# A two-layer decoder trunk: inputs stored in DRAM in the chip's own order

## The chip, the cores and the metric

The kernel runs on one core of a Trainium2 chip. The metric is the time of one execution on the device in microseconds (us), the median of several runs. TensorE is called PE here, its weight loads PEld, VectorE DVE, ScalarE ACT, GpSimd POOL, SyncE SP.

## What is computed

The input is 512 tokens of 1024 features; 16 learned meta tokens are put in front, so T = 528. Two layers follow, each a token mixer and a gated FFN with a causal convolution of width 3, all with residual adds and RMS norms, in float32:

```python
h = concat([meta_tokens, x])                        # (528, 1024)
h = h + diff_attention(rms_norm(h, da_norm), ...)   # 8 heads, two softmaxes each, rope, w_qkv 1024x3072, w_o
h = h + conv_ffn(rms_norm(h, ffn_norm[0]), ...)     # w_up 1024x5632, conv, silu gate, w_down 2816x1024
h = h + dsa_attention(rms_norm(h, dsa_norm), ...)   # indexer picks top keys per query; 16 heads; w_in 1024x3656, w_o
h = h + conv_ffn(rms_norm(h, ffn_norm[1]), ...)
return rms_norm(h, final_norm)[16:]                 # (512, 1024)
```

## The kernel before

**Layout.** The residual stream lies on the chip with features on partitions: eight tiles `h[0]` to `h[7]` of 128 x 528. A projection multiplies weight slabs with them. A slab is 128 output columns of a weight matrix: 8 blocks of 128 x 128, 512 KB, held in `raw` as 128 x 1024 (down projections of the FFN have slabs of 7 or 8 blocks). There are three `raw` buffers.

**Precision.** Every product is done in three passes: a float32 operand is split into a high part (`wh`, rounded by a cast on ACT) and a low part (`wl` = `raw` minus `wh`, on DVE or POOL); `two` issues the pair. `project` then does for each of the 8 blocks six matmuls: high x high, high x low and low x high, each over 272 and 256 columns. Such six are called a step below; a slab is eight steps.

**Loading.** `loader` issues one slab after the other on SP's DMA queue, as `raw` buffers come free; `splitter` issues the casts and subtractions. In DRAM the weights have the order of the reference, so a slab comes as 1024 lines of 512 bytes (`wsrc`). For q and k the columns of a head are permuted so that rope's pairs lie 16 apart; the slab comes in the given order, and `plain(..., perm=True)` permutes while it splits, in two halves of 128 x 512 with strided views. Layer 1's indexer slab (`load_kw`, `parts_kw`) is done in three pieces.

**The start.** `load_tokens` loads x with tokens on partitions, in two halves of four 128 x 512 tiles (`tt`), on ACT's and SP's queues in turn; the 16 meta tokens go to an `ns` tile. For each k of 8, five PE transposes make `h[k]` in PSUM, ACT or DVE copies it out, and `norm.add(k)` makes the high and low part of `h[k]` times the norm's gain (`R`), on ACT and DVE. The sums of squares for the first norm are taken from the token tiles by ten DVE operations (`squares`). PE does 16 transposes of the identity before any data (`warm`). `load_params` loads the gains, the convolution weights and the lambdas as rows, turns them with PE transposes, and copies them to `gcol` and `cw`.

**The order.** Every operation is recorded by generators (tasks) and placed by a planner, class `Plan`, which keeps a modelled clock for each engine and always emits the operation that could start first, with priorities; an `Alt` lets it choose the engine. The real engines then run their rows in that fixed order and wait for each other by semaphores. All operations are recorded on one line (L270 before, L272 after), so that lines say little and tile names much. In the attention stages the planner mixes projection steps with the heads' work on PE: scores (`ps<-K,X`), transposes of the softmax (`ps<-ident,ns`), products with the values (`ps<-ph,R`). `K<-K` is a DMA on POOL's queue which copies half of a key tile to the other partitions; scores wait for it.

**The first norm's chain.** Sums of squares, five PE transposes or none, two POOL operations, then five PE transposes (`ps<-ident,st`, the spread), a copy to `rbc`, two products with the rope tables. After it rope can begin (`e_r`), then the key tiles, `K<-K`, and the first scores.

## Time and profile before

| | |
|---|---|
| median of 3 runs (1418.38 to 1420.27) | 1418.61 us |
| the profiled execution | 1417.88 us |
| its span, first to last instruction | 1416.1 us |
| PE busy | 1372.6 us (97%) |
| DVE, ACT, POOL busy | 960.7, 679.9, 347.5 us |
| DMA engines' mean share | 27.5% of 16 engines for SP's queue, 0.4% for ACT's |
| granted PE clock, mean | 0.989 |

The profiled execution is 0.7 us below the median and 1.8 us above its own span. A busy PE is one that has a matmul under way; where its clock is granted at 0.5 it is busy at half speed (1.2 instead of 2.4 GHz). Idle time of other engines costs nothing by itself.

### The profile page before, as it was taken

Reading aid. Unit: us, or ns where it says so; the run is one execution under the profiler, and the core shown is the slowest. Engines: PE = TensorE matmul, PEld = TensorE weight load, DVE = VectorE, ACT = ScalarE, POOL = GpSimd, SP = SyncE. Lnnn points to the kernel's source line nnn. Section 1 sums busy time; section 2 is a strip of 40 time slices with the busy share of each in tenths; the row PEclk is TensorE's granted clock in tenths of the full one; section 3 lists DMA queues with packets and bytes.
Section 4 is the critical chain, followed back from the end, with each engine's and each line's share of the span. In section 5 each row is a group of like instructions: output and inputs, shape, how many; then the busy total and the mean of one; then the engine's idle time right before and its main releaser. Section 6 shows DMA issues by size and latency. Waiting matters only on the chain. (4 is left out here: it accounts for less than half of the span.)

```text
span 1416.1 us, 26368 instructions
## 1 busy us (share of the span) xinstructions
PE 1372.6 (97%) x10703; PEld 1331.9 (94%) x10703; DVE 960.7 (68%) x1659; ACT 679.9 (48%) x1260; POOL 347.5 (25%) x441
## 2 busy tenths in 40 slices
PE   8989999999999999999989989999999999999997
PEld 7888999999999999999989989898999989989997
DVE  6878767457645763775599988887666637646764
ACT  4566676434423432443356477777444324423454
POOL 1654654420000000000247764442310000000012
PEclk8999999999999999999999999999999999999999
DMA  6422233233233323332312331222333233333333
GB/s 178 103 61 61 76 91 103 57 96 90 81 95 94 87 82 102 90 90 70 90 45 75 83 96 49 69 68 76 94 90 97 80 104 92 91 101 90 90 113 111
DMA packets 223084, 124.33 MB, mean 88 GB/s; under 512 B 7001, under 2 KB 218338, under 8 KB 222962
## 3 DMA queue, kind: packets, MB, share of 16 engines
q1 hardware_dynamic: 219234, 111.89, 27.5%
q0 software_dynamic: 2560, 8.65, 2.9%
q10 hardware_dynamic: 1168, 2.10, 0.4%
q8 instruction: 84, 1.38, 0.4%
q14 instruction: 38, 0.31, 0.1%
HBM read 111.87 MB, written 2.10 MB: 80 GB/s over the span
## 5 line engine op out<-in xcount | busy, mean ns | idle before, releaser
L270 PE MATMUL ps<-R,wh 128*128 128x256 f32 (+4 forms) x4016 | 680.8, 289 | 1.6 <-POOL R L270 0.9
L270 PEld LDWEIGHTS ps<-R,wh 128*128 128x128 f32 (+1 forms) x4016 | 562.5, 189 | 9.4 <-POOL R L270 1.1
L270 PE MATMUL ps<-R,wl 128*128 128x272 f32 (+3 forms) x2008 | 424.4, 288 | 0.0
L270 PE MATMUL ps<-R,K 128*128 128x256 f32 (+3 forms) x3240 | 418.4, 289 | 0.0
L270 PEld LDWEIGHTS ps<-R,K 128*128 128x128 f32 x3240 | 405.6, 189 | 7.6
L270 PEld LDWEIGHTS ps<-R,wl 128*128 128x128 f32 x2008 | 312.2, 188 | 3.2
L270 ACT CAST wh<-raw 128x1024 fp32r<-128x1024 f32 (+3 forms) x173 | 145.6, 847 | 202.7 <-PE ps L270 147.6
L270 DVE TENSOR_TENSOR wl<-raw,wh 128x1024 fp32r<-128x1024 f32 (+3 forms) x128 | 139.9, 1096 | 23.6 <-ACT wh L270 21.8
L270 DVE TENSOR_TENSOR h<-ps,h 128x528 f32<-128x528 f32 (+3 forms) x70 | 45.7, 653 | 143.0 <-PE ps L270 143.0
L270 DVE TENSOR_TENSOR tt<-ps,rbc 128x528 f32<-128x528 f32 (+2 forms) x89 | 62.4, 701 | 114.9 <-PE ps L270 109.6
L270 DVE SCALAR_TENSOR_TENSOR tt<-tt,cw,tt 128x528 f32<-128x528 f32 (+1 forms) x176 | 133.4, 758 | 8.2 <-ACT tt L270 4.9
L270 ACT CAST K<-raw 128x1024 fp32r<-128x1024 f32 (+1 forms) x76 | 77.9, 1027 | 119.9 <-PE ps L270 105.5
L270 POOL TENSOR_TENSOR acc<-acc,tt 128x528 f32<-128x528 f32 (+1 forms) x22 | 36.2, 1645 | 400.6 <-ACT tt L270 400.6
L270 ACT CAST R<-tt 128x512 fp32r<-128x512 f32 (+2 forms) x84 | 48.5, 585 | 139.7 <-DVE tt L270 139.6
L270 DVE TENSOR_TENSOR K<-raw,K 128x1024 fp32r<-128x1024 f32 (+1 forms) x75 | 89.6, 1195 | 10.8 <-ACT K L270 9.3
L270 PE MATMUL ps<-K,X 128*128 128x272 f32 (+2 forms) x464 | 79.7, 308 | 11.0 <-DVE tt L270 5.6
L270 ACT ACTIVATE ns<-ns,st 128x528 f32<-128x528 f32 (+4 forms) x160 | 82.1, 514 | 13.6 <-DVE st L270 11.8
L270 POOL TENSOR_TENSOR wl<-raw,wh 128x512 fp32r<-128x512 f32 (+1 forms) x45 | 70.4, 1566 | 47.6 <-ACT wh L270 47.0
L270 PEld LDWEIGHTS ps<-K,X 128*128 128x128 f32 x464 | 65.6, 182 | 15.9 <-DVE st L270 3.9
L270 ACT ACTIVATE tt<-tt,cw 128x528 f32<-128x528 f32 (+1 forms) x88 | 72.3, 821 | 14.8 <-DVE tt L270 14.6
L270 POOL MEMSET tt<- 128x2 f32 x44 | 4.2, 99 | 302.2 <-DVE tt L270 302.2
L270 ACT ACTIVATE tt<-tt 128x528 f32<-128x528 f32 (+1 forms) x44 | 28.1, 639 | 81.8 <-DVE tt L270 81.7
(120 smaller groups left out, 1359.0 us busy)
## 6 DMA issues: line engine op xcount, KB each, us to landing
raw<-in_ffn_w_up_dram SPq DMA_DIRECT2D x88, 512.0 KB
raw<-in_ffn_w_down_dram SPq DMA_DIRECT2D x32, 448.0 KB
raw<-in_dsa_w_in_dram SPq DMA_DIRECT2D x28, 512.0 KB
raw<-in_da_w_qkv_dram SPq DMA_DIRECT2D x24, 512.0 KB
raw<-in_ffn_w_down_dram SPq DMA_DIRECT2D x22, 512.0 KB
K<-K POOLq DMA_DIRECT2D x32, 264.0 KB, 3.0
raw<-in_da_w_o_dram SPq DMA_DIRECT2D x8, 512.0 KB
raw<-in_dsa_w_o_dram SPq DMA_DIRECT2D x8, 512.0 KB
```

Of the source, the lines that this page charges most:

```text
L270: self.tc.keep_in_program_order(op.call(*op.a, **op.k))
```

## The change

The host now stores all inputs in another order before the launch (`laid_out`), and the kernel reads them in that order:

- Every slab is stored as 128 lines of 4 KB (3.5 KB for slabs of 7 blocks) with the columns of q and k, the indexer's too, already permuted. One DMA of 128 lines takes the place of 1024 lines; the split of every slab is one cast of 128 x 1024 and one subtraction of 128 x 1024.
- Meta tokens and x are stored transposed. `h[k]` is loaded straight as 128 lines of 2112 bytes; the transposes, copies and token tiles are gone. The sums of squares now come from `norm.add` as in the other norms: a square on ACT for each `h[k]`, adds on POOL or DVE, five PE transposes, two DVE reductions.
- Gains, convolution weights and lambdas are stored in the order of `gcol`, `cw` and one `ns` tile: four DMAs, no transposes or copies.
- The loader's first three slabs are issued after `h[0]`, `h[3]` and `h[7]` (`X_SLAB`).

```diff
-    def wsrc(w, r0, nk, c0):
-        return w[r0:r0 + nk * P, c0:c0 + P].rearrange("(k p) c -> p k c", p=P)
...
-            yield sy.dma_start(out=raw[:, :n].rearrange("p (k c) -> p k c", c=P), in_=src)
+            yield sy.dma_start(out=raw[:, :n], in_=src)
...
-            if not perm:
-                yield from two(wh[:, :n], wl[:, :n], raw[:, :n], on=on)
-                return
-
-            ri = raw[:, :n].rearrange("p (c h g i) -> p g c h i", h=2, g=2, i=16)
-            vh = wh[:, :n].rearrange("p (c g h i) -> p g c h i", h=2, g=2, i=16)
-            vl = wl[:, :n].rearrange("p (c g h i) -> p g c h i", h=2, g=2, i=16)
-            for i in range(2):
-                yield from two(vh[:, i], vl[:, i], ri[:, i], on=on)
+            yield from two(wh[:, :n], wl[:, :n], raw[:, :n], on=on)
...
     def load_tokens(norm):
-        q = [s, sy]
-        mt = yield NS
-        yield gains_in
-        yield sy.dma_start(out=mt[:NMETA, :D], in_=A["meta_tokens"])
...
-                yield q[i % 2].dma_start(out=t[:, :512], in_=A["x"][0, i * P:(i + 1) * P, 512 * hf:512 * hf + 512])
...
-            yield [tr(ps[:, TP0 + a:TP0 + b], x, ident[:b - a, :b - a]) for (a, b), x in zip(BLK, ins)]
...
+        yield s.dma_start(out=gcol, in_=A["gains"])
         for k in range(KD):
+            yield (sy, s)[k % 2].dma_start(out=h[k], in_=A["tokens"][k])
+            spawn(norm.add(k), 1)
+            if k in X_SLAB:
+                x_in[X_SLAB.index(k)].set()
+                yield ld[X_SLAB.index(k)]
...
     def load_params():
+        yield x_in[-1]
+        yield ld[2]
+        for l in range(2):
+            yield sy.dma_start(out=cw[l], in_=A["conv"][l].rearrange("p (a b) -> p a b", a=4))
         ns = yield NS
+        yield sy.dma_start(out=ns[:, :256], in_=A["lambdas"])
...
+def laid_out(a):
+    def slabs(w):
+        *l, k, c = w.shape
+        w = w.reshape(*l, k // P, P, c // P, P)
+        n = len(l)
+        return w.transpose(*range(n), n + 2, n + 1, n, n + 3).reshape(*l, c // P, P, k)
```

The planner gives all engines a new order. SP's queue at its very beginning, before:

```order
1 L270 DMA ns_126<-in_meta_tokens_dram 16x1024
2 L270 DMA tt_102<-in_x_dram 128x512
3 L270 DMA tt_104<-in_x_dram 128x512
4 L270 DMA raw_111<-in_da_w_qkv_dram 128x8x128
5 L270 DMA tt_106<-in_x_dram 128x512
6 L270 DMA tt_108<-in_x_dram 128x512
7 L270 DMA raw_112<-in_da_w_qkv_dram 128x8x128
8 L270 DMA raw_113<-in_da_w_qkv_dram 128x8x128
9 L270 DMA ns_127<-in_dsa_norm_dram 8x128
```

And SP's beginning in the changed kernel:

```order
1 L272 DMA h_61<-in_tokens_dram 128x528
2 L272 DMA raw_111<-in_da_qkv_dram 128x1024
3 L272 DMA h_63<-in_tokens_dram 128x528
4 L272 DMA raw_112<-in_da_qkv_dram 128x1024
5 L272 DMA h_65<-in_tokens_dram 128x528
6 L272 DMA h_67<-in_tokens_dram 128x528
7 L272 DMA raw_113<-in_da_qkv_dram 128x1024
8 L272 DMA cw_175<-in_conv_dram 128x176
9 L272 DMA cw_176<-in_conv_dram 128x176
10 L272 DMA ns_126<-in_lambdas_dram 128x256
```

The first row no longer writes an `ns` tile, which POOL clears first; the first slab (`raw_111`) moves from fourth to second place.

ACT's queue just behind its five DMA issues, before (`R` is a high part of a normed `h`, `wh` of a weight slab; `h_61` to `h_68` are `h[0]` to `h[7]`):

```order
7 L270 COPY h_61<-ps_153 128x528
8 L270 COPY h_62<-ps_154 128x528
9 L270 ACTIVATE R_69<-h_61,gcol 128x528
10 L270 CAST wh_114<-raw_111 128x16x32
11 L270 ACTIVATE R_71<-h_62,gcol 128x528
12 L270 ACTIVATE R_73<-h_63,gcol 128x528
13 L270 CAST wh_114<-raw_111 128x16x32
14 L270 ACTIVATE R_75<-h_64,gcol 128x528
```

The same place in the changed kernel (an ACTIVATE into `acc` or `tt` is a square):

```order
7 L272 ACTIVATE R_69<-h_61,gcol 128x528
8 L272 ACTIVATE acc_145<-h_61 128x528
9 L272 CAST wh_114<-raw_111 128x1024
10 L272 ACTIVATE R_71<-h_62,gcol 128x528
11 L272 ACTIVATE R_73<-h_63,gcol 128x528
12 L272 ACTIVATE tt_101<-h_62 128x528
13 L272 ACTIVATE R_75<-h_64,gcol 128x528
14 L272 ACTIVATE tt_102<-h_63 128x528
15 L272 ACTIVATE tt_103<-h_64 128x528
16 L272 CAST wh_116<-raw_112 128x1024
17 L272 ACTIVATE R_77<-h_65,gcol 128x528
18 L272 ACTIVATE R_79<-h_66,gcol 128x528
```

The copies out of PSUM are gone; four squares and the second slab's cast stand ahead of `h[4]`'s high part (`R_77`).

POOL's queue where the first head of layer 0 is made ready, before (`tt`, `X` and `K` belong to rope and the stacked queries and keys, `wl` to a slab):

```order
35 L270 TENSOR_TENSOR tt_105<-tt_105,tt_106 128x528
36 L270 TENSOR_TENSOR wl_115<-raw_111,wh_114 128x16x32
37 L270 TENSOR_TENSOR K_123<-tt_105,K_123 64x528
38 L270 TENSOR_TENSOR wl_115<-raw_111,wh_114 128x16x32
39 L270 DMA K_123<-K_123 64x1056
40 L270 DMA K_125<-K_125 64x1056
41 L270 TENSOR_TENSOR tt_108<-tt_108 16x128
```

The same place in the changed kernel:

```order
36 L272 DMA K_124<-K_124 64x1056
37 L272 MEMSET st_136 128x10
38 L272 TENSOR_TENSOR K_123<-tt_104,K_123 64x528
39 L272 DMA K_123<-K_123 64x1056
40 L272 TENSOR_TENSOR K_125<-tt_104,K_125 64x528
41 L272 DMA K_125<-K_125 64x1056
42 L272 TENSOR_TENSOR tt_107<-tt_107 16x128
```

The slab's subtractions have left POOL here for DVE, and a key subtraction has come to POOL. Over the whole of layer 0's attention, POOL had 4 whole and 12 half subtractions of `wl` and has 1 whole one; DVE had 11 whole and 20 halves and has 30 whole ones. PE has the same 40 steps ahead of its first scores in both kernels; the spread stands behind 17 of them before, behind 18 now.

## Rows read from the trace of the kernel before

**Rows 1.** The page's first part: busy time, share of the span, instructions.

```profile
span 1416.1 us, 26368 instructions
PE 1372.6 (97%) x10703; PEld 1331.9 (94%) x10703; DVE 960.7 (68%) x1659; ACT 679.9 (48%) x1260; POOL 347.5 (25%) x441
```

**Rows 2.** Busy time by stretch: the start, layer 0's attention, its FFN, layer 1's attention, its FFN, the end. Columns: stretch, its length, busy us (and instructions) of PE, PEld, DVE, ACT, POOL, granted PE clock, DMA share, GB/s.

```profile
0.00:36.00 36.00, 30.29 (x194) 27.07 (x195) 22.29 (x54) 14.35 (x24) 5.49 (x23) 0.86 0.62 181
36.00:283.00 247.00, 232.95 (x1818) 224.31 (x1817) 184.10 (x397) 151.41 (x359) 139.11 (x153) 0.99 0.30 78
283.00:700.00 417.00, 417.00 (x3431) 416.93 (x3430) 245.90 (x306) 151.98 (x195) 16.93 (x58) 1.00 0.31 89
700.00:1000.00 300.00, 283.91 (x2199) 272.82 (x2198) 258.24 (x594) 196.70 (x468) 156.22 (x184) 0.98 0.26 68
1000.00:1380.00 380.00, 380.00 (x2830) 363.04 (x2830) 233.96 (x287) 149.43 (x190) 19.30 (x13) 1.00 0.33 97
1380.00:1416.10 36.10, 28.44 (x241) 27.73 (x239) 16.18 (x25) 16.01 (x28) 10.41 (x10) 0.93 0.35 114
```

**Rows 3.** The timeline of the first 55 us, the rows that mark the path (start us, length, engine, operation, count, idle time before and what ended it).

```profile
0.72 0.58 ACTq L270 DMA_DIRECT2D ns<-in_da_norm_dram  x1
1.34 1.81 ACTq L270 DMA_DIRECT2D tt<-in_x_dram  x4
1.79 3.51 PE L270 MATMUL ps<-ident 128*128 128x128 f32 x16 [1.79 <-POOL ident masks.py:199]
3.17 1.28 ACT L270 ACT_TABLE_LOAD   x1 [3.17 <-issue]
4.09 0.39 SPq L270 DMA_DIRECT2D ns<-in_meta_tokens_dram  x1
10.43 0.47 PE L270 MATMUL ps<-ident,tt 128*128 128x128 f32 x1 [1.38 <-DMA tt<-in_x_dram]
18.11 0.98 PE L270 MATMUL ps<-R,wh 128*128 128x272 f32 x4
22.50 0.65 PE L270 MATMUL ps<-R,wh 128*128 128x272 f32 x4
23.24 0.65 PE L270 MATMUL ps<-R,wh 128*128 128x272 f32 x4
25.38 0.40 PE L270 MATMUL ps<-R,wl 128*128 128x272 f32 x2
25.61 0.24 PE L270 MATMUL ps<-ident,ns 88*128 88x88 f32 x1
32.43 0.71 PE L270 MATMUL ps<-ident,st 128*128 128x128 f32 x5
51.50 1.34 PE L270 MATMUL ps<-K,X 128*128 128x272 f32 x8 [1.56 <-DMA K<-K]
```

**Rows 4.** What SP's queue waited for in the first 36 us (total, times, longest).

```profile
SPq L270 <- POOL ns L270: 3.7, 1, 3.7
```

**Rows 5.** Single microseconds and the loading stretch of the start; columns as in rows 2.

```profile
2.00:3.00 1.00, 1.00 (x6) 1.00 (x6) 0.00 (x0) 0.00 (x0) 1.00 (x3) 1.00 0.49 90
3.00:15.40 12.40, 8.48 (x37) 6.35 (x36) 5.60 (x16) 5.09 (x8) 1.49 (x10) 0.72 0.98 291
10.00:18.00 8.00, 7.57 (x30) 5.47 (x31) 6.24 (x15) 5.99 (x11) 0.00 (x0) 0.50 0.77 211
18.00:19.00 1.00, 1.00 (x8) 1.00 (x7) 1.00 (x2) 1.00 (x2) 0.00 (x0) 0.67 0.64 196
```

**Rows 6.** The page's DMA queues: packets, MB, share of 16 engines over the span. q1 is SP's queue (nearly all of it lines of 512 bytes), q10 ACT's (x and the outputs, lines of 2 KB).

```profile
q1 hardware_dynamic: 219234, 111.89, 27.5%
q10 hardware_dynamic: 1168, 2.10, 0.4%
```

**Rows 7.** Operations by form over the whole span (count | busy us, mean ns of one | idle before).

```profile
L270 ACT ACTIVATE tt<-h 128x528 f32<-128x528 f32 x21 | 13.1, 630 | 0.0
L270 ACT CAST wh<-raw 128x1024 fp32r<-128x1024 f32 x82 | 86.1, 1050 | 135.0 <-PE ps L270 101.0 <-issue 33.8
L270 ACT CAST wh<-raw 128x512 fp32r<-128x512 f32 x72 | 43.6, 615 | 37.3 <-PE ps L270 17.7 <-issue 12.8 <-POOL R L270 3.6
L270 DVE TENSOR_TENSOR wl<-raw,wh 128x1024 fp32r<-128x1024 f32 x74 | 92.0, 1243 | 16.2 <-ACT wh L270 15.2
L270 DVE TENSOR_TENSOR wl<-raw,wh 128x512 fp32r<-128x512 f32 x35 | 29.6, 851 | 6.5 <-ACT wh L270 6.1
L270 POOL TENSOR_TENSOR wl<-raw,wh 128x1024 fp32r<-128x1024 f32 x8 | 19.5, 2436 | 5.0 <-ACT wh L270 4.9
L270 POOL TENSOR_TENSOR wl<-raw,wh 128x512 fp32r<-128x512 f32 x37 | 50.9, 1378 | 42.6 <-ACT wh L270 42.1
L270 POOL TENSOR_TENSOR acc<-acc,tt 128x528 f32<-128x528 f32 x13 | 23.3, 1794 | 54.3 <-ACT tt L270 54.3
```

**Rows 8.** Operations by form in the first 30 us.

```profile
L270 DVE SCALAR_TENSOR_TENSOR R<-h,gcol,R 128x528 fp32r<-128x528 f32 x8 | 5.8, 764 | 0.0
L270 ACT ACTIVATE R<-h,gcol 128x528 fp32r<-128x528 f32 x8 | 5.6, 732 | 0.0
```

**Rows 9.** The longest wait of PE in layer 1's attention, from its timeline, and the stretch around it (columns as in rows 2).

```profile
732.79 2.79 PE L270 MATMUL ps<-K,X 128*128 128x400 f32 x10 [3.12 <-DVE tt L270]
730.00:740.00 10.00, 7.21 (x35) 7.20 (x36) 9.81 (x17) 3.73 (x9) 3.96 (x3) 0.66 0.20 54
```

More of the change, by code (lines that the diff above doesn't have):

```diff
@@ L44 @@
 NK = 72
+GROUPS = [range(0, 7), range(7, 14), range(14, 22)]
 SPARE, SPARE_TAKEN, SPARE_FFN = 800.0, 600.0, 0.0
 AHEAD = 3
+X_SLAB = (0, 3, 7)
 WO = 3
@@ L763, in attention0 @@
     def attention0(norm, nxt):
-        W = A["da_w_qkv"][0]
         order = [x for hd in range(8 + LAG) for x in ((hd, 0), (hd, 1), (hd - LAG, 2)) if 0 <= x[0] < 8]
-        w_qkv = [plain(wsrc(W, 0, KD, c * D + hd * P), KD, perm=c < 2) for hd, c in order]
-        w_o = [plain(wsrc(A["da_w_o"][0], 0, KD, m * P), KD) for m in range(KD)]
+        w_qkv = [plain(A["da_qkv"][8 * c + hd]) for hd, c in order]
+        w_o = [plain(A["da_o"][m]) for m in range(KD)]
         e_r, e_f = Event(), Event()
@@ L1400, in load_params @@
         got_params.set()
-    got_gains, got_params, gains_in, x_half, x_in = (Event() for _ in range(5))
+    got_params = Event()
+    x_in = [Event() for _ in X_SLAB]
     class Final:
@@ L1509 @@
     arrays, args = {}, {}
-    given = {n: np.ascontiguousarray(inputs[n]) for n in _INS}
+    given = laid_out({n: np.asarray(inputs[n]) for n in _INS})
     given["rope"] = rope_tables()
```

156 lines of the change are left out of this document (39 added, 117 removed).

## The prediction

> **What bounds the kernel.** I read the busy times first, then the busy times by stretch, then the timeline of the start. PE is busy 1372.6 of 1416.1 us [rows 1]. By stretch [rows 2] both FFNs keep PE busy without a gap (417.0 of 417.0 and 380.0 of 380.0 us): nothing that the change does to DMA, ACT, DVE or POOL can shorten these 797 us, since PE's own work there stays the same. PE's 43.5 idle us lie in four places: 5.7 in the first 36 us, 14.0 in layer 0's attention, 16.1 in layer 1's, 7.7 at the end. The end is left alone (its PE rows stand in the same order). So the change can act on the start and on the two attentions.
>
> At the start the loss is larger than the idle time. PE's first real work, the first step of the first projection, begins at 18.11 us [rows 3]. Before that it does most of the 40 transposes of x, on a granted clock of 0.50 [rows 5]. The last matmuls of the first slab end at 25.38 + 0.40 = 25.8 us [rows 3]. From there PE has no gap up to the first scores at 51.50, where it waits 1.56 us for `K<-K`. Whatever brings the end of the first slab forward brings all later work forward.
>
> **The start, step by step.** *Issues.* SP's first DMA waited 3.7 us for POOL to clear its tile [rows 4] and went out at 4.09 us [rows 3]. A load of `h[0]` waits for nothing, so SP can begin as ACT does, at about 0.7. With 0.45 us an issue (four took 1.81 us [rows 3]) ACT's five are out by 3.2 and SP's seven by 3.9 us.
>
> *Transfers.* Eight `h` tiles of 270 KB and three slabs of 524 KB are 3.74 MB, as many bytes as before. Before, they ran at 291 GB/s from 3.0 to 15.4 us with the DMA engines full (share 0.98) [rows 5]. ACT's queue with its 2 KB lines took 0.4% of 16 x 1416.1 us for 2.10 MB: 23.2 GB/s an engine, 371 in all. SP's queue with its 512-byte lines gives 287 by the same sum [rows 6]. Bytes began to move about 1.2 us after the first big issue (1.34, against a share of 0.49 in the third microsecond [rows 3, 5]), so from 1.9 us now. All has moved by 12.0 (at 371) or 14.8 us (at 291); the last token tile, with one slab behind it, by 10.6 or 13.0. For the completion I add 1 us, my choice. I take the faster rate, because every line is now at least 2112 bytes long. The first slab stands second on SP; with what ACT's queue moves beside it, it is in at about 6 us.
>
> A rule of the Trainium skill speaks against this step: DMA: Bandwidth & Descriptors, Specifications, gives 512 bytes as the smallest transfer for line rate. By it longer lines win nothing, and the slow rate stays. The trace disagrees so far, 287 against 371 GB/s [rows 6]. By the rule the sum below would lose 0.4 us and no more, because ACT and not DMA sets the end.
>
> *ACT.* Its table load ends at 4.45 us [rows 3]. In its new order it does the high part of `h[0]` (0.73 [rows 8]) and one square (0.63 [rows 7]), to 5.8, and waits for the slab, to 6. Then up to the high part of `h[7]` come two slab casts of 1.05 [rows 7], seven high parts and three squares: 2.1 + 5.1 + 1.9 = 9.1, to 15.1 us. With the slow rate `h[6]` lands at 14.0, when ACT wants it at 13.6: this is the 0.4 us.
>
> *DVE and PE.* DVE's low part follows each high part (0.76 [rows 8]), the last by 16.0. A step of PE at full clock is 23.24 - 22.50 = 0.74 us [rows 3]. So the first slab ends at 16.7 us at full clock.
>
> *Clock.* PE's warm-up transposes end at 5.3 us. Before, with the gaps that followed, the clock stood at 0.50 from 10 to 18 us and came back in the nineteenth, though PE worked on from 10.43 [rows 3, 5]: 7.9 us. Now PE does single steps between waits from 7 to 11 us, then waits for `h[4]` until 12.9 + 0.8 = 13.7. If the clock is low from there for 7.9 us again, the last four steps take 1.48 each (+2.9) and 2.0 us of the next slab run at half speed (+1.0): 3.9 us. If it stays up, nothing. I take the middle, 2.0: an effective end of the first slab at 18.7.
>
> *What follows.* Up to the first scores both kernels have 40 steps. Behind the first slab two parameter transposes of 0.24 go and five of the square sums come (like the spread's five, 0.71 [rows 3]): 0.2 us lost. The sums have to be ready: ACT's last four squares end at 17.6; a chain of adds follows, three of them on POOL at 1.79 [rows 7], done at about 21. PE is there five steps after the slab, at 22.4; at full clock it would wait 0.6. From the spread to the first scores were 51.50 - 32.43 = 19.1 us [rows 3], a chain of DVE and POOL work. PE now covers it with 22 steps instead of 23, so its wait for `K<-K` grows by 0.7.
>
> Gain at the start: 25.8 - 18.7 - 0.2 - 0.7 = **6.2 us**. Bounds: 8.2 with the clock up; 2.9 with the clock low throughout (1.9 more), the slow rate (0.4) and the first slab 1 us later.
>
> **The attentions.** 36 permuted slabs are split whole. On ACT two casts of 0.615 become one of 1.05, 0.2 us less; on DVE two of 0.85 become one of 1.24; on POOL two of 1.38 become one of 2.44 [rows 7]. In exchange a whole subtraction holds its engine longer at a stretch. In layer 0 POOL loses nearly all its subtractions, and DVE takes them; the planner pays with chain work (keys, sine products) that goes to POOL. The new order shifts every head against the steps that cover it. I cannot read from an order which of the 30.1 idle us [rows 2] shrink or grow, and take 0. The unit of both bounds is the longest wait: 3.12 us for DVE, after which the clock stood at 0.66 over ten microseconds, 6.8 us at half speed, so 3.4 more: 6.5 us for one such wait [rows 9].
>
> Slabs that land faster save nothing elsewhere: in no stretch behind the start does PE wait for `raw`, and the FFNs cover the transfers with full PE (DMA share 0.31 to 0.33 [rows 2]). If that cover were gone, a 512 KB slab at 287 GB/s would cost 1.8 us.
>
> **Sum.** The profiled execution took 1417.9 us, its span 1416.1. 1417.9 - 6.2 = 1411.7. The median of the runs lies 0.7 above this execution, so 1412.4.
>
> **Rivals.** *The attentions give it back* (13%): the new order opens one more wait with a low clock, 1412.4 + 6.5 = 1418.9. For it: the chain work that POOL takes over in layer 0. Against it: DVE and ACT have less to do in total.
>
> *The attentions gain too* (13%): one such wait goes, 1405.9. For it: the longest wait is for DVE, while DVE was full (9.81 of 10 us [rows 9]), and the indexer's slabs there cost DVE less.
>
> *Slower* (6%): whole subtractions on POOL. Layer 1's attention had halves there and now has wholes of 2.44 us; a sine product, a key or `K<-K` issue queued behind one is late by up to 1.06 us more than behind a half, and PE with it once its cover is short. Two waits of the size of rows 9 opened there cost 13 us, and the time is 1412.4 + 13 = 1425. One alone leaves it at the first rival's 1418.9; from two on the kernel is slower.
>
> *The start does not come forward* (4%): tokens and slabs share the DMA engines so that the last token tile lands with the last slab, 14.8 + 1; then 0.73 + 0.76 + 0.74 behind it, 18.0, and a low clock: end at 21.9, gain 3.0 or less, 1415.8 to 1417.
>
> **Numbers.** The forecast holds 64%, with its own range of 1408 to 1415.7. A change under 0.2% (2.8 us) can hardly be told from none here. Faster: 64 + 13 = 77%. Same: the first and the last rival, 17%. Slower: 6%. For 8 in 10 I leave out the slower case and the outer parts of the rivals on each side: 1405.5 to 1418.5.
>
> **What would show it.** In the new trace: SP's first issue before 1.5 us; the DMA share near 1 from 2 us on, ending by 12 to 13; the first projection step at 7 to 9, the first slab's last matmul between 16.7 and 20.6; the spread near 27 and the first scores near 45; FFN stretches of 417 and 380 us unchanged. PE's idle time in the attentions should be 14 and 16 us within 3 each. The prediction is wrong if the first slab ends after 21, or if the attentions' lengths (247 and 300 us) move by more than 4.

## The result, and the profile after

The changed kernel takes 1429.05 us (median of 1427.81 to 1430.32) against 1418.49 of the kernel before beside it: a ratio of 1.0074 [1.0059, 1.0089], slower by 10.6 us. The forecast was 1412.4, faster by 6. The profiled execution took 1429.84 us, its span is 1428.0.

The page's first part for the changed kernel, and its row of SP's queue (packets, MB, share of 16 engines), against [rows 1, 6]:

```profile
span 1428.0 us, 26125 instructions
PE 1373.3 (96%) x10662; PEld 1334.3 (93%) x10662; DVE 958.7 (67%) x1613; ACT 677.1 (47%) x1221; POOL 332.3 (23%) x432
q1 hardware_dynamic: 32544, 111.84, 25.6%
```

PE has 41 instructions fewer and is busy 0.7 us longer; DVE, ACT and POOL all have fewer instructions and less busy time than before. The packets on SP's queue fell from 219234 to 32544 for the same bytes. So no engine has more operations, and yet the end lies 11.9 us later.

The changed kernel by stretch (start, layer 0's attention, its FFN, layer 1's attention, its FFN, end; columns as in rows 2):

```profile
0.00:36.00 36.00, 30.35 (x205) 29.26 (x206) 23.91 (x35) 16.53 (x24) 14.79 (x28) 0.95 0.52 187
36.00:280.00 244.00, 224.16 (x1721) 215.32 (x1720) 170.33 (x368) 147.97 (x345) 132.24 (x153) 0.97 0.27 73
280.00:700.00 420.00, 420.00 (x3454) 419.79 (x3453) 248.11 (x304) 153.01 (x189) 18.87 (x59) 1.00 0.30 91
700.00:1000.00 300.00, 279.53 (x2139) 268.83 (x2138) 259.94 (x591) 189.35 (x440) 136.56 (x170) 0.97 0.25 69
1000.00:1380.00 380.00, 379.02 (x2824) 361.89 (x2823) 233.45 (x286) 146.24 (x183) 15.24 (x10) 1.00 0.30 92
1380.00:1428.00 48.00, 40.27 (x332) 39.25 (x330) 22.95 (x33) 24.03 (x42) 14.63 (x13) 0.96 0.39 121
```

Against [rows 2] PE's idle time is 19.8 us in layer 0's attention (14.0 before) and 20.5 in layer 1's (16.1), and the granted clock is 0.97 in both (0.99 and 0.98).

The changed kernel's timeline at the places of [rows 3] (start, length, engine, line, operation, count, idle time before it and what ended it); the row at 26.91 is the spread, the one at 306.93 the first of the sums for layer 0's FFN norm, and the last two are layer 1's first scores and its first head's values:

```profile
0.73 0.39 SPq L272 DMA_DIRECT2D h<-in_tokens_dram  x1
7.28 1.25 PE L272 MATMUL ps<-R,wh 128*128 128x272 f32 x4 [1.81 <-ACT wh L272]
14.90 0.81 PE L272 MATMUL ps<-R,wh 128*128 128x272 f32 x2 [2.04 <-DVE R L272]
18.09 0.40 PE L272 MATMUL ps<-R,wl 128*128 128x272 f32 x2
26.91 0.71 PE L272 MATMUL ps<-ident,st 128*128 128x128 f32 x5
45.53 1.35 PE L272 MATMUL ps<-K,X 128*128 128x272 f32 x8 [1.86 <-DMA K<-K]
...
306.93 0.71 PE L272 MATMUL ps<-ident,acc 128*16 128x128 f32 x5
...
720.87 0.39 PE L272 MATMUL ps<-K,X 128*128 128x272 f32 x1 [1.11 <-ACT K L272]
...
848.50 0.56 PE L272 MATMUL ps<-zt,zv 128*128 128x16 f32 x2
```

The first slab ends at 18.5 us and the first scores begin at 45.53, 6.0 us earlier than in [rows 3]. That gain is then given back twice. Five marks, read from the timelines (us from the span's start), place the losses. L0 norm is PE's first row of the sums for the FFN norm of layer 0, L1 norm that of layer 1:

| mark | before | changed | difference |
|---|---|---|---|
| first scores, layer 0 | 51.50 | 45.53 | -6.0 |
| L0 norm | 304.06 | 306.93 | +2.9 |
| first scores, layer 1 | 716.29 | 720.87 | +4.6 |
| first head's values, layer 1 | 834.50 | 848.50 | +14.0 |
| L1 norm | 1032.56 | 1044.50 | +11.9 |

Layer 0's attention loses 8.9 us. Layer 1 loses 9.1 between L0 norm and L1 norm: 1.7 ahead of its first scores, 9.4 from there to its first head's values, while DVE finds the top keys, and 2.1 are won back behind them.

### The profile page after: what moved, and what is told of

Its sections match the earlier page's. It is cut to its first block, busy times and chain, and to the rows that moved or that the text cites. A ratio compares the mean times of both kernels' runs of the same rounds, so it can differ in the third digit from the quotient of the medians.

```text
span 1428.0 us, 26125 instructions
## 1 busy us (share of the span) xinstructions
PE 1373.3 (96%) x10662; PEld 1334.3 (93%) x10662; DVE 958.7 (67%) x1613; ACT 677.1 (47%) x1221; POOL 332.3 (23%) x432
## 3 DMA queue, kind: packets, MB, share of 16 engines
q1 hardware_dynamic: 32544, 111.84, 25.6%
## 4 chain that ended last, share of the span: by engine, by line
PE 68%; DVE 10%; ACT 2%; issue 1%; POOL 0%; POOLq 0%; ACTq 0%; DVEq 0%
PE ps L272 68%; DVE tt L272 3%; DVE acc L272 3%; DVE st L272 2%; DVE wl L272 1%; DVE ns L272 1%; ACT tt L272 0%; ACT ns L272 0%; DVE K L272 0%; DVE pl L272 0%; ACT K L272 0%; DVE X L272 0%; ACT ph L272 0%; POOL tt L272 0%; DVE zt L272 0%
## 5 line engine op out<-in xcount | busy, mean ns | idle before, releaser
L272 PE MATMUL ps<-R,K 128*128 128x272 f32 (+3 forms) x3264 | 430.9, 290 | 0.0
L272 PEld LDWEIGHTS ps<-R,K 128*128 128x128 f32 x3264 | 412.9, 189 | 8.4
L272 ACT CAST wh<-raw 128x1024 fp32r<-128x1024 f32 (+1 forms) x134 | 138.5, 1034 | 174.4 <-PE ps L272 135.5
L272 DVE TENSOR_TENSOR wl<-raw,wh 128x1024 fp32r<-128x1024 f32 (+1 forms) x124 | 158.4, 1278 | 25.6 <-ACT wh L272 24.2
L272 POOL TENSOR_TENSOR acc<-acc,tt 128x528 f32<-128x528 f32 (+1 forms) x25 | 40.9, 1638 | 415.0 <-ACT tt L272 412.7
L272 DVE TENSOR_TENSOR K<-raw,K 128x1024 fp32r<-128x1024 f32 (+1 forms) x76 | 91.4, 1203 | 13.3 <-ACT K L272 12.0
L272 POOL TENSOR_TENSOR tt<-tt,Sr 128x528 f32<-128x528 f32 x28 | 42.2, 1510 | 117.1 <-DVE tt L272 117.1
```

The costliest lines, as they stand in the source:

```text
L272: self.tc.keep_in_program_order(op.call(*op.a, **op.k))
```

## The experiments

Three theories stood at first. **Theory 1**: whole splits (128x1024 instead of two of 128x512) cost the time. **Theory 2**: the planner's new order costs it, whatever made the planner draw another one. **Theory 3**: the transfers in 4 KB lines cost or win time by themselves.

The table has all runs but the changed kernel itself. "Layer 0" is the time of L0 norm, "layer 1" the stretch from L0 norm to L1 norm, both of the one profiled execution. Kernels whose rows are the same in layer 0 differ by up to 3.6 us there between executions (300.51 and 296.93), in layer 1 by 1.4 (729.25 and 730.62), so smaller differences in these columns say nothing. The profiled execution is also not always near the median: it lies 3.3 us above it for nudge_after_dve, 4.6 below it for new_order_pieces, and 2 to 3 below it for l1_pieces, nudge_before_dve, nudge_after_pe and nudge_pieces_dve. The kernel before took 1418.6 to 1419.1 beside these runs (medians); its columns are 304.06 and 728.50, those of the changed kernel 306.93 and 737.57.

| run | start | splits | order | us | ratio [interval] | layer 0 | layer 1 |
|---|---|---|---|---|---|---|---|
| layout_same_order | old | pieces | old | 1419.22 | 1.0005 [0.9995, 1.0014] | 305.05 | 729.08 |
| start_only | new | pieces | drawn anew | 1413.80 | 0.9967 [0.9955, 0.9979] | 300.51 | 729.25 |
| slabs_only | old | whole | drawn anew | 1428.35 | 1.0071 [1.0056, 1.0086] | 304.53 | 737.33 |
| after_halves | new | contiguous halves | drawn anew | 1421.49 | 1.0021 [1.0012, 1.0031] | 304.23 | 731.58 |
| l1_pieces | new | pieces in layer 1 | drawn anew there | 1419.84 | 1.0007 [0.9987, 1.0027] | 304.44 | 728.30 |
| l1_pool | new | whole, q and k of layer 1 on POOL | drawn anew there | 1433.74 | 1.0107 [1.0077, 1.0136] | 306.72 | 742.33 |
| nudge_after_dve | new | whole | nudged | 1419.33 | 1.0003 [0.9992, 1.0014] | 304.66 | 732.84 |
| nudge_after_pe | new | whole | nudged | 1420.15 | 1.0012 [0.9998, 1.0026] | 300.40 | 731.74 |
| nudge_after_act | new | whole | nudged | 1425.49 | 1.0051 [1.0028, 1.0074] | 303.68 | 736.64 |
| nudge_before_dve | old | pieces | nudged | 1427.68 | 1.0074 [1.0055, 1.0093] | 308.90 | 731.76 |
| nudge_before_pe | old | pieces | nudged | 1429.26 | 1.0080 [1.0051, 1.0109] | 307.45 | 735.77 |
| nudge_before_act | old | pieces | nudged | 1422.76 | 1.0030 [1.0015, 1.0044] | 309.01 | 729.66 |
| old_order | new | pieces | old, replayed | 1414.97 | 0.9978 [0.9968, 0.9988] | 301.01 | 728.86 |
| old_order_whole | new | whole | old, replayed | 1419.29 | 1.0008 [0.9999, 1.0017] | 298.25 | 734.84 |
| all_pieces | new | pieces | that of start_only | 1413.25 | 0.9966 [0.9953, 0.9979] | 296.93 | 730.62 |
| nudge_pieces_dve | new | pieces | nudged | 1418.93 | 1.0001 [0.9991, 1.0012] | 300.03 | 731.62 |
| new_order_pieces | new | pieces | changed kernel's, replayed | 1428.02 | 1.0057 [1.0043, 1.0072] | 303.58 | 734.57 |
| old_order_mix | new | whole in layer 0, pieces in layer 1 | old, replayed | 1413.65 | 0.9968 [0.9954, 0.9982] | 298.32 | 730.41 |

### The lines alone

The slabs of the kernel before come from the new layout; the splits keep their pieces, so that each engine's rows stand as before.

```diff
-            yield sy.dma_start(out=raw[:, :n].rearrange("p (k c) -> p k c", c=P), in_=src)
+            yield sy.dma_start(out=raw[:, :n], in_=src)
...
+                ri, vh, vl = (x[:, :n].rearrange("p (c g h i) -> p g c h i", h=2, g=2, i=16) for x in (raw, wh, wl))
...
-            ri = raw[:, :n].rearrange("p (c h g i) -> p g c h i", h=2, g=2, i=16)
```

Expected of layout_same_order: 

> The kernel before with nothing but the slabs' place in DRAM changed: lines of 4 KB, columns already permuted. The splits keep their pieces (two strided halves for q, k and the indexer), the tokens are loaded as before, and every row on PE, ACT, DVE and POOL stands where it stood in the kernel before. Theory 1 (whole splits cost time: a subtraction of 128x1024 on DVE and POOL instead of two of 128x512) and theory 2 (the planner's new order costs time, whatever moved it) both expect the time of before, 1418.5 +- 1.5 us, and the same waits of PE in both attentions. Theory 3 (the transfers in 4 KB lines cost or win time themselves, since they land earlier and collide with other work) expects a difference of more than 2 us, up to the 10.5 us lost if it is all of the cause.

Measured: 1419.22 us, within 0.2% of before. Theory 3 falls as a cause. The 4 KB lines cost nothing and win nothing where PE covers the transfers.

### The start alone, the slabs alone, the pieces back

start_only takes the changed kernel and puts the slabs back as they were; slabs_only takes the kernel before and gives it the new slabs, whole splits included; after_halves takes the changed kernel and splits the permuted slabs in two contiguous halves:

```diff
         def parts(raw, wh, wl):
+            if halves:
+                for a in (0, 512):
+                    yield from two(wh[:, a:a + 512], wl[:, a:a + 512], raw[:, a:a + 512], on=on)
+                return
             yield from two(wh[:, :n], wl[:, :n], raw[:, :n], on=on)
```

Expected of start_only: 

> The changed kernel with the slabs as before: 512-byte lines, q, k and the indexer's slabs split in permuted halves. Only the start (tokens, gains, convolution weights, lambdas) is new. Theory 1 (whole splits): the start's 6 us are kept, 1412.5 us (1411 to 1414), no wait above 3.2 us in layer 1's top keys. Theory 2 (order): the start's gain of 6 us at the first scores is there, and the attentions then lose or win by an amount of their own, several us, that has nothing to do with halves: any time from 1405 to 1425. The start itself (3, lines): if the 512-byte slabs at 287 GB/s held it back, the first scores come later than 45.5 by 1 us or more.

Expected of slabs_only: 

> The kernel before with the slabs of the changed kernel (4 KB lines, whole splits everywhere) and the old start. Theory 1 (whole splits): the changed kernel's loss in the attentions without the gain of the start, 1418.5 + 10.5 + 6 = 1435 us (1431 to 1438), with the loss in the last heads of layer 0 (some 5 us) and in layer 1 between the first scores and the first head's values (some 10 us). Theory 2 (order): a new order with a loss or gain of its own, anything from 1410 to 1435, and not in these two places.

Expected of after_halves: 

> The changed kernel, all in the new layout, with one thing undone: q, k and indexer slabs of the first 36 permuted ones are split in two contiguous halves of 128x512 again. Theory 1 (whole splits): 1412.5 us (1411 to 1415), layer 1's stage from the first scores to the first head's values back at the length of before, 118 us instead of 128. Theory 2 (order): a third order, with a loss of its own; the time lies anywhere from 1405 to 1430, and no nearer to 1412 than slabs split whole do.

Measured: 1413.80, 1428.35 and 1421.49 us. The start alone is faster by 4.8 us (1413.80 against 1418.63), its first scores at 44.03. slabs_only loses in layer 1 what the changed kernel loses (737.33 against 737.57), and in the same place, which theory 2 had not expected, but nothing in layer 0 (304.53), and it stays below theory 1's 1431 to 1438. So layer 0's loss needs the new start and the new slabs together, which speaks for order, and layer 1's follows the slabs. after_halves did not come back to 1412. Layer 1 came back for the most part (731.58), though its stretch from the first scores to the first head's values took 124.3 us, not the 118 of theory 1. Layer 0 gave its gain away once more, with other waits (from the first scores to L0 norm 5.2 us of PE's waits are for `K<-K`, 2.7 in the changed kernel). Theory 1 alone is wrong.

### Layer 1 by itself

l1_pieces undoes the whole splits in layer 1 only. l1_pool keeps them whole but lets POOL alone subtract layer 1's q and k slabs:

```diff
-        on = (g, v) if len(slabs) > 1 else (v,)
+        on = only or ((g, v) if len(slabs) > 1 else (v,))
...
-        w_qkv = [plain(A["dsa_qkv"][8 * c + m]) for m, c in order]
+        w_qkv = [plain(A["dsa_qkv"][8 * c + m], (g,) if c < 2 else None) for m, c in order]
```

Expected of l1_pieces: 

> The changed kernel with layer 1's slabs alone split in strided halves as before (indexer in three pieces); layer 0 keeps whole splits. So far: the layout alone changed nothing (1419.2), old start with whole splits lost its time in layer 1 (728.5 us between the two FFN norms before, 737.3 there, 737.6 in the changed kernel), new start with old splits has 729.3 there. Theory 1 (whole splits, for layer 1): that stretch comes back to 729 +- 1.5 and the time to 1429 - 8.5 = 1420.5 us; layer 0 stays as in the changed kernel, its FFN norm at 306.9 +- 0.5. Theory 2 (any new order has its own loss): that stretch lies anywhere from 727 to 740.

Expected of l1_pool: 

> The changed kernel with whole splits, but layer 1's q and k slabs may be subtracted on POOL alone, so DVE loses them. Theory 1a (whole splits cost because DVE, which is full while it finds the top keys, got two more slabs' subtractions, and they are stretched while POOL works): DVE's stretch from the first scores to the first head's values shrinks from 127.6 to about 120, the time to 1421 +- 2 us. Theory 1b (the size itself: whole subtractions of 2.4 us stand before POOL's chain work): the stretch grows, 1431 us or more. Theory 2 (order): anywhere from 1420 to 1435.

Measured: l1_pieces has 728.30 in layer 1 and 1419.84 us, as theory 1 said (1420.5); its L0 norm at 304.44 lies outside the 306.9 +- 0.5 expected. l1_pool has 742.33 and 1433.74: theory 1a, that DVE only has to be freed of the slabs, falls in this form, and the stretch grew to 133.3 us, as theory 1b expected. DVE has only 2 slabs there, and is still busy for 125.6 of the 133.3 us, so the number of its slabs alone does not set its time. PE's waits in l1_pool (releaser; total, times, longest) have a new row:

```profile
PE ps L272 <- POOL wl L272: 6.8, 2, 3.7
```

POOL's 13 whole subtractions in that stage take 2.4 us each, and PE waits for two of them.

### Nudges: what an order is worth

Six controls change no operation at all. One number of the planner's model moves by 0.5 or 3 ns, in the changed kernel and in the kernel before:

```diff
-            return n / (1.92 if fast else 0.96) + 69 + 60 * (ptr > 0 and "reduce" not in name)
+            return n / (1.92 if fast else 0.96) + 72 + 60 * (ptr > 0 and "reduce" not in name)
```

The nudges called pe make `n / 2.4 + 3` into `n / 2.4 + 3.5`, those called act add 3 to an ACT operation.

Expected of nudge_after_dve: 

> A control for the order: the changed kernel with one number of the planner's model moved by nothing that matters, DVE's fixed cost of an operation from 69 to 72 ns. No operation is added, removed or resized, but the planner's choices differ from the first heads on. Theory 1 (whole splits): the stretch between the two FFN norms stays at 737 +- 2 us and layer 0's FFN norm at 307 +- 2; 1429 +- 3 us. Theory 2 (order): both move by several us, the sum by 5 or more in either direction.

Expected of nudge_before_dve: 

> The same control on the kernel before: DVE's fixed cost in the planner's model 72 instead of 69 ns, nothing else. Theory 1: 1418.5 +- 3 us, 728.5 +- 2 between the FFN norms. Theory 2 (and the constants of the planner were fitted to one order): several us slower than before, 1422 to 1432, as every disturbed order of this kernel would be.

Expected of nudge_after_pe: 

> Second control of the changed kernel's order: in the planner's model a matmul costs 0.5 ns more, nothing else. So far between the two FFN norms (layer 1): slabs in pieces 728.3 to 731.8 us in six kernels, the nudged kernel before among them, whole slabs 732.8 (changed kernel, DVE nudged) and 737.3 to 737.6. Theory 1+2 (whole splits cost some 4 to 9 us in layer 1, and the order scatters each layer by some 4 us): 732 to 740 here, and layer 0's FFN norm at 302 to 309. Theory 2 alone (order only): 728 to 740, as likely near 729 as near 737.

Expected of nudge_after_act: 

> Third control of the changed kernel's order: in the planner's model an ACT operation costs 3 ns more, nothing else. Theory 1+2: 732 to 740 us between the FFN norms, layer 0's FFN norm at 302 to 309. Theory 2 alone: 728 to 740, as likely near 729 as near 737. The time of the whole in either case 1415 to 1432.

Expected of nudge_before_pe: 

> Second control of the order of the kernel before: a matmul costs 0.5 ns more in the planner's model, nothing else. The first such control took 1427.7 us, with layer 0's FFN norm at 308.9 instead of 304.1 and 731.8 instead of 728.5 in layer 1. Theory 1+2: 728 to 733 in layer 1, layer 0 at 303 to 310; slower than before by 2 to 10 us if the constants of the planner were fitted to the one order. Theory 2 alone: layer 1 as high as 737 too.

Expected of nudge_before_act: 

> Third control of the order of the kernel before: an ACT operation costs 3 ns more in the planner's model, nothing else. Theory 1+2: 728 to 733 us between the FFN norms, layer 0's FFN norm at 303 to 310. Theory 2 alone: layer 1 as high as 737 too. 1419 to 1428 as a whole.

Measured: the changed kernel's work takes 1429.05, 1419.33, 1420.15 or 1425.49 us, that of the kernel before 1418.6, 1427.68, 1429.26 or 1422.76. A nudge that means nothing moves the time by up to 10.2 us (1429.26 against 1419.07 beside it), as much as the change did. The means of the four are 1423.5 and 1424.6 us: over these few orders no difference between the kernels can be told. The kernel before is the fastest of its four and the changed kernel the slowest of its four. Layer 1 lies at 728.5 to 735.8 with pieces and 731.7 to 737.6 with whole splits, so by its length the splits can't be told from the order; theory 1's 737 +- 2, expected of nudge_after_dve, would have failed in two of the three nudged changed kernels. The stretch from layer 1's first scores to its first head's values does part them: 118.2 to 121.5 us with pieces, 123.6 to 127.6 with whole splits, in one execution each. The expectation that nudged kernels before would be slower, since their constants were fitted to one order, held in its direction three times out of three.

### The order held fixed

The decisive runs take the choice from the planner. The sequence of tasks on each engine is recorded from one kernel and replayed in another; only the tokens, the slab loads, the parameters and the first norm's chain are still placed by the model.

```diff
+                if t.key:
+                    at = [(self.rows[x[1].eng][self.next[x[1].eng]], x) for x in at
+                          if self.next[x[1].eng] < len(self.rows[x[1].eng])]
+                    at = sorted(((n[0], x) for n, x in at if n[1] == t.key), key=lambda y: y[0])[:1]
+                    if not at:
+                        continue
```

Expected of old_order: 

> New start, new layout in 4 KB lines, slabs split in strided pieces, and from the first projection on every engine's rows in the order of the kernel before, written down and replayed instead of chosen by the planner (only the tokens, the norm's gains, the parameters and the first norm's chain are placed by the planner). If the attentions lost their time to a new order alone, this is the sum of the prediction with its zero made true: the start's 6 us kept to the end, layer 0's FFN norm at 304.5 - 6 = 298.5 +- 1, 728.5 to 729.3 between the FFN norms, 1412.5 +- 1.5 us as a whole. If an earlier start loses its time to something else (the planner's old order is only right for the old start, say, because the chain behind the first norm is no shorter), layer 0's FFN norm lies at 301 or later and the time above 1415.

Expected of old_order_whole: 

> As old_order, with the pieces of every slab merged: one cast in the place of the first piece's cast, one subtraction of 128x1024 in the place and on the engine of the last piece's subtraction; every other row stands where it stands there. This is the changed kernel's work in the old order. If whole splits cost nothing by themselves and only the order did harm: within 1.5 us of old_order, 1412.5. If whole splits cost by themselves: layer 1 longer by 3 to 9 us, 732 to 738 between the FFN norms, and 1416 to 1421 us.

Expected of new_order_pieces: 

> The changed kernel with every engine's rows in the order that it has, written down and replayed, but each whole split of a q, k or indexer slab taken apart in place: the strided pieces' casts one behind the other where the one cast stood, their subtractions where the one subtraction stood and on its engine. If order and whole splits add: 1429.05 - 4.3 = 1424.7 +- 2 us, and 730 to 733 us between the FFN norms. If the new order itself holds the whole loss of layer 1 (its chain work and its engines): 1428 or more, 736 to 738, since two halves cost DVE even more (2 x 0.85 against 1.24 us). If the new order loses only where whole splits stand in it: 1420 or less.

Measured, all with the new start and 4 KB lines (medians in us):

| | pieces | whole splits |
|---|---|---|
| order of the kernel before | 1414.97 | 1419.29 |
| order of the changed kernel | 1428.02 | 1429.05 |

The order costs 13.1 us with pieces and 9.8 with whole splits. Whole splits cost 4.3 us in the old order, as old_order_whole's second case had it (1416 to 1421, layer 1 at 732 to 738), and 1.0 in the new, where the intervals overlap. So the order is the main cause; that the two do not add is likely but not certain. An order here is the row on each engine and also the choice of engine; the replay fixes both and does not part them. For new_order_pieces the third case (1420 or less, a loss only where whole splits stand in the order) is refuted, and the second fits by the time: the new order holds the loss itself. The sum of both (1424.7 +- 2) lies below the median, but its upper part is inside the interval (1424.9 to 1429.1 us). The profiled execution of this kernel was the fastest of its four by 3.8 us, so its columns in the large table flatter it.

The top-key stretch of layer 1 shows it most clearly, in one execution each. From the first scores to the first head's values it takes 118.8 us in old_order and 118.9 in old_order_whole, 126.3 in new_order_pieces and 127.6 in the changed kernel: the order decides there, and whole splits add at most 1.3. What whole splits cost in the old order falls behind that stretch, from the first head's values to L1 norm (202.3 us in old_order_whole, 197.9 in old_order).

old_order missed its 1412.5 by 2.5 us, in the start; its L0 norm at 301.01 and its 1414.97 us lie at the edge of the second case that it had named. PE waits for ACT and DVE at the first slabs. Its timeline:

```profile
8.02 1.25 PE L390 MATMUL ps<-R,wh 128*128 128x272 f32 x4 [2.56 <-ACT wh L390]
18.93 0.72 PE L390 MATMUL ps<-ident,acc 128*16 128x128 f32 x5 [2.06 <-DVE acc L390]
21.21 0.81 PE L390 MATMUL ps<-R,wl 128*128 128x272 f32 x2 [1.07 <-DVE wl L390]
```

Its first scores stand at 48.80, against 45.66 in old_order_whole; from there to L0 norm both take the same (252.2 and 252.6). Pieces alone do not make the start late, since start_only and all_pieces have pieces too and first scores at 44.03 and 44.23; what in the replayed order does was not separated. So in the old order whole splits help at the start and hurt in layer 1, and the last replay puts each where it helps.

Expected of old_order_mix: 

> Old order replayed, new start and layout, whole splits in layer 0 and strided pieces in layer 1. If whole splits cost in layer 1 alone: layer 0's FFN norm at 298.3 +- 1, 728.9 +- 1 between the FFN norms, 1412.4 +- 1.5 us: the prediction's figure. If the difference of the two old-order kernels in layer 0 (2.8 us in one look each) was chance: 1415.

Measured: 1413.65 us (1411.53 to 1418.49), layer 0 at 298.32, layer 1 at 730.41. This is within 1.3 us of the forecast (1412.4), with layer 1 above the 728.9 +- 1 expected. The start's gain is kept through layer 0 and in part through layer 1: 6.4 us at the first scores, 5.7 at L0 norm and 3.8 at L1 norm. Whole splits in layer 1 alone, the one difference to old_order_whole, cost 5.6 us.

### A version that beats both

all_pieces is the changed kernel with the strided pieces put back, in the new layout; its rows are those of start_only.

Expected of all_pieces: 

> The changed kernel whole, new start and all slabs in 4 KB lines, with the strided pieces of before: on every engine the rows of start_only, so only the 4 KB lines differ from that. start_only took 1413.8. If the lines are worth nothing (as in the first run): 1413.8 +- 1.5. If they help the start, where they land earlier: up to 1.5 us less, 1412.3.

Expected of nudge_pieces_dve: 

> Control of all_pieces: DVE's fixed cost in the planner's model 72 instead of 69 ns, nothing else. If 1413.8 was a lucky draw: 1416 to 1424, layer 0's FFN norm anywhere from 300 to 307. If pieces with the new start are faster in most orders: below 1416.

Measured: 1413.25 us, 0.9966 [0.9953, 0.9979], the fastest kernel run here by its median, together with old_order_mix and start_only, from which its interval does not part it. It is no proof that pieces win in every order: nudged, it takes 1418.93, no different from before.

## Where the time goes in the new order

**Layer 0.** Columns as in rows 2; the stretch from the first scores to L0 norm of the changed kernel, and the same of old_order_whole, which has the same operations in the old order:

```profile
45.50:306.90 261.40, 243.39 (x1876) 234.60 (x1876) 174.48 (x374) 153.45 (x352) 134.06 (x153) 0.97 0.28 78
```

```profile
45.60:298.20 252.60, 239.37 (x1876) 230.24 (x1877) 178.75 (x385) 150.80 (x348) 132.60 (x141) 0.99 0.29 80
```

PE has the same 1876 matmuls in both. The changed kernel needs 8.8 us more: 4.8 of idle time (18.0 against 13.2) and 4.0 of longer busy time at a clock of 0.97 instead of 0.99. Nearly every idle microsecond is paid twice, once as a wait and once as slow work behind it. The clock behind PE's longest wait of this stretch (3.3 us, to 50.90) shows the second part, columns as in rows 2:

```profile
51.00:52.00 1.00, 1.00 (x10) 0.95 (x10) 1.00 (x2) 0.97 (x2) 0.85 (x2) 1.00 0.00 0
53.00:54.00 1.00, 1.00 (x7) 1.00 (x6) 0.04 (x2) 1.00 (x4) 0.61 (x2) 0.50 1.00 187
56.00:57.00 1.00, 1.00 (x11) 0.95 (x10) 0.56 (x5) 1.00 (x4) 0.39 (x3) 1.00 0.37 55
```

PE's waits in this stretch, two rows of each kernel (the second pair is old_order_whole):

```profile
PE ps L272 <- POOL st L272: 6.8, 7, 2.2
PE ps L272 <- ACT tt L272: 3.3, 1, 3.3
```

```profile
PE ps L389 <- POOL st L389: 5.0, 4, 2.3
PE ps L389 <- ACT tt L389: 1.5, 3, 1.0
```

The longest shows how an order makes a wait. ACT's and PE's rows around 50 us in the changed kernel:

```profile
48.78 0.63 ACT L272 CAST K<-tt 64x528 fp32r<-64x528 f32 x1 [6.03 <-DVE tt L272]
49.32 1.04 ACT L272 CAST wh<-raw 128x1024 fp32r<-128x1024 f32 x1
50.26 0.59 ACT L272 COPY tt<-ps 128x528 f32<-128x528 f32 x1
50.90 0.71 PE L272 MATMUL ps<-ident,tt 128*16 128x128 f32 x5 [3.29 <-ACT tt L272]
```

PE wants the copy. ACT is idle from 42.75 on, and PE's last step of the fifth slab ends at 43.67, so by these rows the copy could run some 6 us earlier (an estimate; whether its buffer was free by then is not shown). But a key's cast stands ahead of it in the row and waits 6.03 us for DVE, and then the whole cast of 1.04 us stands there too.

**Layer 1.** From the first scores to the first head's values DVE is the bound, since it finds the top keys. Columns as in rows 2; the changed kernel, and old_order:

```profile
720.00:848.50 128.50, 113.78 (x839) 110.86 (x839) 121.93 (x293) 72.23 (x169) 77.77 (x95) 0.92 0.26 75
```

```profile
713.00:832.00 119.00, 109.22 (x841) 106.75 (x841) 115.10 (x281) 69.00 (x166) 78.24 (x95) 0.97 0.26 72
```

DVE is busy 121.9 of 128.5 us and 115.1 of 119.0. It has 6.8 us more to do, POOL 0.5 less, and the stretch is 9.5 longer: 4.9 of PE's idle time and 4.6 of longer busy time, at a clock of 0.92 instead of 0.97. The subtractions of `wl` in these stretches (ns, minimum, median and maximum; first and last start; forms), the first two rows of the changed kernel, the others of old_order:

```profile
L272 DVE TENSOR_TENSOR wl<-raw,wh x8: 1208/1633/2347, 719.4 to 833.1; 128x1024 fp32r<-128x1024 f32 x8
L272 POOL TENSOR_TENSOR wl<-raw,wh x7: 2384/2396/2412, 752.5 to 796.9; 128x1024 fp32r<-128x1024 f32 x7
```

```profile
L390 POOL TENSOR_TENSOR wl<-raw,wh x15: 1277/1297/2401, 746.0 to 827.3; 128x512 fp32r<-128x512 f32 x11, 128x1024 fp32r<-128x1024 f32 x4
L390 DVE TENSOR_TENSOR wl<-raw,wh x8: 674/1198/1818, 713.0 to 830.6; 128x512 fp32r<-128x512 f32 x5, 128x1024 fp32r<-128x1024 f32 x3
```

In the old order DVE does 5.5 slabs there and POOL 9.5; in the new one DVE does 8 and POOL 7. The slabs' subtractions are 4.1 of DVE's 6.8 us more (13.3 against 9.2 us busy). The timeline of PE in the changed kernel shows who is late when the top keys are done:

```profile
816.80 0.81 PE L272 MATMUL ps<-R,wl 128*128 128x272 f32 x2 [2.30 <-DVE wl L272]
827.06 1.25 PE L272 MATMUL ps<-K,X 128*128 128x272 f32 x4 [3.05 <-DVE st L272]
838.50 1.97 PE L272 MATMUL ps<-ident,ns 128*128 128x128 f32 x8 [3.85 <-DVE pl L272]
```

All three releasers are DVE. In new_order_pieces, which has the same engines for the same slabs, the last two are there too (3.41 and 4.49 us).

Why the planner gave DVE more slabs can be read in its code; this is an argument, since no run changed it alone. It takes the engine with the smaller modelled end and adds `SPARE`, 800 ns, to DVE's until the last block's top keys are found. A half costs 602 ns on DVE and 1202 on POOL in the model, so 1402 against 1202: POOL, if both are free. A whole costs 1136 and 2354, so 1936 against 2354: DVE. The constant stood for half a slab; merging the halves doubled the difference that it is weighed against. The counts fit that: over the whole kernel POOL's subtractions fell from 37 halves and 8 wholes [rows 7] to 10 wholes, and between 715 and 846 us DVE has 8 or 9 slabs and POOL 7 in the changed kernel and all three of its nudges, against 5.5 or 6 and 9 or 9.5 in the three nudges of the kernel before. l1_pool's opposite extreme was no better; whether a division between them is best was not tried.

## Why the prediction was wrong, point by point

- **What bounds the kernel**: right. The FFN's stretch stays full (420.00 of 420.00 us), and from L0 norm to layer 1's first scores there are 413.9 us, 412.2 before.
- **The start**: right in size and mostly in its steps. First issue at 0.73 (0.7 forecast), first slab's end at 18.5 (18.7), first scores 6.0 us earlier (6.2). One step was off: DMA is full until 17 us (mean share 1.00 from 2 to 17) and not until 12 or 13, because further slabs and the rope tables follow at once. The low clock came as granted 0.79 from 14 to 15 us and 0.50 from 15 to 18, shorter than the 7.9 us of the upper case.
- **The rule of the Trainium skill** (DMA: Bandwidth & Descriptors, Specifications: 512 bytes as the smallest transfer for line rate) was set against the trace with the right outcome. With the DMA engines full, the changed kernel moves 388 GB/s from 3 to 13 us (share 1.02), where the kernel before moved 291 [rows 5]:

```profile
3.00:13.00 10.00, 8.04 (x38) 6.97 (x36) 6.46 (x9) 9.25 (x14) 3.21 (x10) 1.00 1.02 388
```

  The prediction's own sum for 371 against 287 was weaker than it looked: by the same sum over the whole run SP's queue gives 306 GB/s with its longer lines (111.84 MB in 25.6% of 16 x 1428.0 us). At one order the longer lines were worth nothing, with the old start (layout_same_order) and with the new (first scores at 44.03 us in start_only, 44.23 in all_pieces), as the prediction's 0.4 us let expect.
- **The attentions at 0**: this step failed. "I cannot read from an order which of the 30.1 idle us shrink or grow, and take 0", with bounds of 6.5 us. The attentions lost 8.9 + 9.1 us. In the order of the kernel before the zero would have been right for layer 0, whose stretch is 252.6 us in old_order_whole and 252.6 before. For layer 1 it would have been right with pieces only (old_order_mix, 1413.65): the whole splits, which the prediction also put at nothing, cost 5.6 us there, and the changed kernel's work in the old order takes 1419.29. The larger part that was missed is that the order of before is not a mean draw. Its planner's numbers seem to suit it: of the eleven other orders that the planner drew here for a whole kernel (l1_pieces and l1_pool, drawn anew in layer 1 alone, left out), ten lie at 1418.9 to 1429.3 us and one (start_only's) at 1413.8. The three nudges of the kernel before lost 8.9, 10.2 and 3.7 us against the kernel before beside them, 7.6 in the mean; with that in the place of the 0 the sum would have been 1420.0 (an estimate from runs made afterwards), still 9 us short.
- **The bound of that step** was too narrow because it priced one more wait in all. Here a new order opened several, and the slow clock behind them nearly doubled them: 4.8 + 4.0 and 4.9 + 4.6 us.
- **The rival "slower"** (6%) had the wrong engine for this kernel. It put whole subtractions on POOL. They went to DVE, and in layer 1 DVE was full [rows 9]. Where POOL was made to take them (l1_pool) PE did wait for them, and the time was longer still. The prediction had both facts, that DVE takes slabs over from POOL and that DVE is the bound while it finds the top keys, but it added them only for layer 0 and counted DVE's total as falling. The rival that gives the gain back (13%) had the mechanism and less than half of the size (6.5 us, where the time came out 16.7 above the forecast).
- **What would show it**: the attentions' lengths moved by more than 4 us, the condition that the prediction named for being wrong. A slip without effect: in the last rival a gain of 3.0 us gives 1415.6, not 1415.8.

Open: which of the rows in layer 0's new order cost the most was not separated, nor, in layer 1, the choice of engine from the order of the rows, and the bias was not run at another value with whole splits.

## What to carry to other kernels

Where a planner draws the whole order, any edit draws a new one, and the new draw alone can move the time by as much as the edit: replay the old order to see what the edit is worth, and nudge a number that means nothing to see what a draw is worth. Constants tuned to one piece size (here a bias between two engines) are worth a second look when the piece size changes, first in the stage where the favoured engine is already full. An idle microsecond of PE in the two attentions here cost nearly two, with the granted clock at 0.50 behind the longer waits.

## What the runs showed of the hardware

In the rows below, an operation of DVE with two tensor inputs stands still while POOL's operation runs, and POOL's while DVE's does; DVE's MATCH_REPLACE8, a part of the search for the top keys, is not touched. DVE in the changed kernel around 800 us:

```profile
796.90 0.41 DVE L272 MATCH_REPLACE8 acc<-st,acc 128x256 f32<-128x256 f32 x1
801.59 0.41 DVE L272 MATCH_REPLACE8 acc<-st,acc 128x256 f32<-128x256 f32 x1
804.21 0.70 DVE L272 TENSOR_TENSOR tt<-tt,Cr 128x528 f32<-128x528 f32 x1
805.94 2.35 DVE L272 TENSOR_TENSOR wl<-raw,wh 128x1024 fp32r<-128x1024 f32 x1
808.41 1.61 DVE L272 TENSOR_TENSOR tt<-tt,Cr 128x528 f32<-128x528 f32 x1
```

And POOL there:

```profile
796.94 2.40 POOL L272 TENSOR_TENSOR wl<-raw,wh 128x1024 fp32r<-128x1024 f32 x1 [1.17 <-ACT wh L272]
805.88 1.33 POOL L272 TENSOR_TENSOR tt<-tt,Sr 128x528 f32<-128x528 f32 x1 [6.49 <-DVE tt L272]
807.28 2.18 POOL L272 TENSOR_TENSOR tt<-tt,tt 128x528 f32<-128x528 f32 x1
```

The product with `Cr` takes 0.70 us with POOL idle and 1.61 beside it. Take the rows as turns: POOL's product ends at 807.2, then DVE's subtraction runs (at least 1.21 us long, as above) to 808.4, then POOL's next (1.33 for a product of its size) to 809.7, then DVE's product (0.70) to 810.4. The trace ends them at 807.21, 808.29, 809.46 and 810.02, in this order and a little earlier. MATCH_REPLACE8 takes 0.41 beside POOL (796.90) and without it (801.59). The Trainium skill states this rule (SBUF — State Buffer, SBUF: two separate sides): a DVE operation with two inputs in SBUF and a GpSimd operation that reads SBUF take turns at a shared pair of ports, and the later one blocks for the whole of the other. The trace agrees, within 0.5 us over three turns. By the trace, then, a subtraction that goes from POOL to DVE costs DVE more than its own time as long as POOL has other work: in the layer 1 stage the eight whole ones on DVE have a median of 1.63 us against a minimum of 1.21.
